# Attention scores on 128 rows in both matmuls, value products that alternate between column halves, and GpSimd's arithmetic on VectorE, in a hybrid decoder layer

## The chip, the cores and the metric

The kernel runs on one core of a Trainium2 chip. The metric is the device time of one execution in microseconds, the median of several runs. Five engines work side by side, each on its own queue of instructions in order: PE (TensorE, with weight loads listed apart as PEld), DVE (VectorE), ACT (ScalarE), POOL (GpSimd) and SP (SyncE, which here only issues DMAs). They meet through semaphores.

## The reference

One decoder layer over 2048 positions of width 1024. After an RMSNorm one projection feeds two groups of heads: four HGRN2 heads (a recurrence in chunks) and eight attention heads of width 64 with two key-value heads, a sliding window of 128 and a learned sink in the softmax. Both outputs are concatenated and projected, then comes a gated MLP with a causal depthwise convolution, then a last RMSNorm. The part that the change touches most:

```python
def sliding_window_attention_with_sinks(q, k, v, sinks):
    qb = q.reshape(B, nb, ATT_BLOCK, ATT_KV_HEADS, ATT_GROUP, ATT_HD)
    kb, vb = band_keys(k), band_keys(v)          # own and previous block of 128 keys
    scores = jnp.einsum('bnqhgd,bnkhd->bnhgqk', qb, kb) * scale
    scores = jnp.where(mask[None, :, None, None], scores, -jnp.inf)
    m = jnp.maximum(jnp.max(scores, axis=-1, keepdims=True), sink)
    p = jnp.exp(scores - m)
    denom = jnp.sum(p, axis=-1, keepdims=True) + jnp.exp(sink - m)
    return jnp.einsum('bnhgqk,bnkhd->bnqhgd', p / denom, vb)
...
proj = rmsnorm(h, norm_mix_w) @ w_in
h = h + jnp.concatenate([o_hg, o_att], -1) @ w_out
v = rmsnorm(h, norm_ffn_w)
h = h + (silu(conv(v @ w_gate)) * (v @ w_up)) @ w_down
return rmsnorm(h, final_norm_w)
```

## The kernel before

The 2048 positions go through in two halves of 1024 (`hf`). Each half has the same stages: the first projections of keys and values, four rounds of heads (in round `h` one HGRN2 head, `hgrn`, and one attention step, `attend`, that handles one query head of each key-value head), the output projection (`out_proj`), gate and up (`gate_up`), and `down`. Activations lie transposed, features on the 128 partitions and positions along the free dimension.

Products with weights keep float32 precision by splitting both factors into a high part that is rounded to the matmul type (a cast on ACT) and the low rest (a subtraction). A product is then high x high, high x low and low x high. The low part of a weight tile is made in `prep` (L177), that of an activation in `split` (L205) and `split_into` (L554). Before the change these subtractions run on POOL unless the caller names VectorE; so do the low part of q (L330) and the gate's product with its sigmoid (L441). A raw weight tile, its high part and its low part turn in rings of three, two and two tiles, so the load, the cast and the subtraction of a tile wait until PE is done with an earlier one.

`unit` (L180) is one projection of 128 output features: 48 matmuls of 512 columns. `project_v` makes the values of two HGRN2 heads with matmuls of 256 columns (`pvv`, L545 to L547).

In `attend`, `qT` holds the 64 features of one query head in partitions 0 to 63 and those of a head of the other key-value group in 64 to 127 (`rows(kv)`). `KS[r, kv]` holds the high part of the keys in the 64 rows of that group and the low part in the other 64. So one matmul with 128 rows, of a `qh` whose high part stands in both halves, gives high x high plus high x low (L341), and a second one with the 64 rows of `ql` and of the high keys gives low x high (L343). A bank of PSUM (`psc`, from the two banks of the kind "at") takes two query blocks of 128, each against 256 keys; ACT copies the previous block's scores out (L350) and VectorE lays the own block's over them under a mask (L351). `qh` is a tile of the ring of raw weights (`RAW` = 3), `ql` one of the ring "pp" (four tiles), which later holds the masked probabilities `po` and `pp`. After the softmax PE transposes the probabilities (L378), VectorE masks them (L381), and the value products (L389 for the own block, L392 for the previous one) write the 64 output features of each key-value head to its own half of PSUM's partitions, so each uses 64 of the array's 128 columns. Their factors are plain float32, and the trace shows two records for each such product. Key-value head 0's eight products come first, then head 1's.

The HGRN2 head ends with a reciprocal root (`rsqrt`, L150 to L160, a chain of a dozen steps on VectorE over 8 elements a partition), a scaling (L520) and a transpose on PE (`pot`, L525).

The order of the instructions on each engine is not the order of the code. A scheduler with a model of the engines' times lays them out when the program is built, within the dependences; after that each engine runs its list in order. So a change of a few lines moves instructions over long stretches. The generators of `hgrn` and `attend`, advanced by the main loop (L949 to L976), give the order that the scheduler starts from.

Of the kernel before, what the change touches and what calls it, by code (L numbers as in the profile page):

```python
# [8 lines left out]
F32 = mybir.dt.float32  # L9
F32R = mybir.dt.float32r  # L10
# [3 lines left out]
ALU = mybir.AluOpType  # L14
# [3 lines left out]
P = 128  # L18
# [27 lines left out]
def hymba_layer(ctx: ExitStack, tc: tile.TileContext, a: dict, out: bass.AP):  # L46
# [122 lines left out]
    def prep(src, slots=False, parts=(slice(0, D),)):  # L169

        raw = raw4(None)
        hi, lo = [hp.tile([P, D], F32R, tag="m", name=f"w{t}", bufs=KT) if slots else
                  wp.tile([P, D], F32R, tag=t, name=f"w{t}", bufs=2) for t in ("hi", "lo")]
        for c in parts:
            nc.sync.dma_start(raw[:, c], src[:, c])
            nc.scalar.copy(hi[:, c], raw[:, c])  # L176
            nc.gpsimd.tensor_tensor(lo[:, c], raw[:, c], hi[:, c].bitcast(F32), op=ALU.subtract)  # L177
        return hi, lo

    def unit(src, X, name, order=range(KT), kind="mm", then={}):  # L180
# [19 lines left out]
    def split(src, w=None, eng=None, dst=None):  # L200

        h, l = dst or new_x()
        if w is None:
            nc.scalar.copy(h, src)
            (eng or nc.gpsimd).tensor_tensor(l, src, h.bitcast(F32), op=ALU.subtract)  # L205
        else:
            nc.scalar.activation(h, src, AF.Identity, scale=w)
            nc.vector.scalar_tensor_tensor(l, src, w, h.bitcast(F32), op0=ALU.mult, op1=ALU.subtract)
        return h, l
# [68 lines left out]
    def rows(kv):  # L278
        return slice(kv * HD, (kv + 1) * HD)
# [32 lines left out]
    def attend(hf, j, X, invb, KS, V, mix, p):  # L312
# [8 lines left out]
        for g in range(NB):  # L321
            sc = p.tile([P, 2, 4, P], F32, tag="sc", name="sc", bufs=2)
            gs = slice(g * 512, (g + 1) * 512)
            qh = wp.tile([P, 2, 512], F32R, tag="raw", name="qh", bufs=RAW)
            ql = p.tile([P, 512], F32R, tag="pp", name="ql", bufs=4)
            for kv in range(2):
                r, other = rows(kv), rows(1 - kv)
                nc.scalar.copy(qh[r, kv], qT[r, gs])
                nc.scalar.copy(qh[other, kv], qT[r, gs])
                nc.gpsimd.tensor_tensor(ql[r], qT[r, gs], qh[r, kv].bitcast(F32), op=ALU.subtract)  # L330
            for i0 in (0, 2):
                for kv in range(2):
                    r = rows(kv)
                    pb = ps("at", "psc")
                    first = hf == 0 and g == 0 and i0 == 0
                    for i in range(2):
                        n = g * 4 + i0 + i
                        w0 = 1 if first and i == 0 else 0
                        o = pb[:, i * 256 + w0 * P:(i + 1) * 256]
                        ks = slice((n + w0) * P, (n + 2) * P)  # L340
                        nc.tensor.matmul(o, qh[:, kv, (i0 + i) * P:(i0 + i + 1) * P], KS[:, kv, ks],  # L341
                                         start=True, stop=False)
                        nc.tensor.matmul(o, ql[r, (i0 + i) * P:(i0 + i + 1) * P], KS[r, kv, ks], start=False, stop=True)  # L343
                    pv = pb.rearrange("p (i w k) -> p i w k", i=2, w=2)
                    dst = sc[:, kv, i0:i0 + 2]
                    if first:
                        nc.vector.memset(dst[:, 0], NEG)
                        nc.scalar.copy(dst[:, 1], pv[:, 1, 0])
                    else:
                        nc.scalar.copy(dst, pv[:, :, 0])  # L350
                    nc.vector.copy_predicated(  # L351
                        dst, C.own.bitcast(U32).unsqueeze(1).to_broadcast([P, 2, P]), pv[:, :, 1])
# [19 lines left out]
        for g, sc in enumerate(scs):  # L372
# [7 lines left out]
                for dst, mk in zip(pm[kv], (C.ownT, C.prevT)):  # L380
                    nc.vector.tensor_tensor(dst, ptv, mk.unsqueeze(1).to_broadcast([P, 4, P]), op=ALU.mult)  # L381
            oT = ps("at", "poT")
            for kv in range(2):
                r = rows(kv)
                po, pp = pm[kv]
                for i in range(4):
                    n = g * 4 + i
                    noprev = hf == 0 and n == 0
                    nc.tensor.matmul(oT[r, i * P:(i + 1) * P], V[:, n + 1, r], po[:, i],  # L389
                                     start=True, stop=noprev)  # L390
                    if not noprev:
                        nc.tensor.matmul(oT[r, i * P:(i + 1) * P], V[:, n, r], pp[:, i],  # L392
                                         start=False, stop=True)
            gs = slice(g * 512, (g + 1) * 512)
            if j < ATT_J - 1:
                nc.scalar.copy(qT[:, gs], oT)
# [9 lines left out]
    def hgrn(hf, h, X, invb, vs, WG, mix, p, fu=None):  # L406
# [28 lines left out]
        def gate():  # L435
            gu = unit(WG.get(h, a["w_g"][h]), X, "g")
            s = p.tile([P, HALF], F32, tag="f", name="sg", bufs=2)
            for b, bs in halves():
                nc.vector.tensor_tensor(q[:, bs], gu[b], invb[:, bs], op=ALU.mult)
                nc.scalar.activation(s[:, bs], q[:, bs], AF.Sigmoid)  # L440
                nc.gpsimd.tensor_tensor(q[:, bs], q[:, bs], s[:, bs], op=ALU.mult)  # L441

        if h == HG - 1:
            gate()
# [106 lines left out]

    def split_into(h, l, src, eng=None):
        nc.scalar.copy(h, src)  # L553
        (eng or nc.gpsimd).tensor_tensor(l, src, h.bitcast(F32), op=ALU.subtract)  # L554

    class Operands:

# [486 lines left out]
```

## Time and profile before

| | us |
|---|---|
| median of three runs | 2345.15 |
| lowest and highest of the three | 2342.76 and 2345.19 |
| the profiled execution, and its span | 2339.59 and 2337.7 |
| mean granted clock of PE | 0.985 |
| heads of the first half, about | 40 to 440 |
| output projection of the first half, about | 440 to 523 |
| gate and up, then down, of the first half | 523 to 940, 940 to 1166 |

A row of the groups gives line, engine, operation, the tile written and the tiles read, the form and the count; behind the first bar the busy time in us and the mean of one in ns; behind the second the idle time of the engine just before such instructions and what ended it. A row of the timeline gives the start and the length in us and the same names; rows of one kind that follow each other closely are merged (`x2`). Matmuls overlap in the array, so how fast they go is read from the distance of their starts, not from their lengths. `128*64` before the form of a matmul is the number of array rows and columns that it uses.

### The profile page before, as it was taken

The numbers are of one execution on the slowest core, as the hardware profiler recorded it, in microseconds if no ns is written. First come the engines' busy times: TensorE is split into PE (matmuls) and PEld (weight loads), VectorE is DVE, ScalarE is ACT, GpSimd is POOL, SyncE is SP. The second block draws the span as 40 slices with busy tenths as digits, with TensorE's granted clock in tenths as the row PEclk, the third lists the DMA queues.
The fourth block names the chain that finished last, engine by engine and source line by source line (L and its number), as shares of the span: only waits on it lengthen the run. The fifth ranks groups of instructions, "written<-read, shape, count | busy, mean of one in ns | idle before, by whom it ended". The sixth has DMA issues, their size and how long they took to land.

```text
span 2337.7 us, 29813 instructions
## 1 busy us (share of the span) xinstructions
PE 2293.0 (98%) x11622; PEld 1907.0 (82%) x11622; DVE 1630.1 (70%) x2307; ACT 1008.1 (43%) x1735; POOL 295.4 (13%) x176
## 2 busy tenths in 40 slices
PE   8999998999999999999999999999999999999997
PEld 6988987877888888888788879878778888888887
DVE  6446465588788887885854463665888788877866
ACT  5334334254444443534633253343554444453353
POOL 3212215041000000000112122151400000000000
PEclk9999998999999999999999999999999999999999
DMA  4001001142232323883630010012323232349743
GB/s 145 19 28 46 10 28 36 51 152 92 86 117 86 126 81 131 333 297 127 214 115 28 19 46 10 28 55 92 116 77 114 98 113 91 117 144 377 246 138 122
DMA packets 87693, 254.19 MB, mean 109 GB/s; under 512 B 10752, under 2 KB 12928, under 8 KB 87552
## 3 DMA queue, kind: packets, MB, share of 16 engines
q1 hardware_dynamic: 85248, 251.17, 31.4%
q8 instruction: 91, 1.49, 0.3%
q10 hardware_dynamic: 2304, 1.12, 0.2%
q14 instruction: 50, 0.41, 0.1%
HBM read 195.10 MB, written 57.15 MB: 108 GB/s over the span
## 4 chain that ended last, share of the span: by engine, by line
PE 93%; DVE 4%; ACT 2%; issue 1%; DMA 1%; POOL 0%; SPq 0%; ACTq 0%; DVEq 0%; POOLq 0%
PE X L656 7%; PE X L658 7%; PE X L657 7%; PE pop L193 6%; PE f L193 4%; PE q L193 4%; PE hq L193 4%; PE Y L656 3%; PE Y L658 3%; PE Y L657 3%; PE g L193 3%; PE pdx L839 3%; PE plev L456 3%; PE pdx L840 3%; PE pdx L841 3%; PE pdy L840 3%
## 5 line engine op out<-in xcount | busy, mean ns | idle before, releaser
L177 POOL TENSOR_TENSOR wlo<-raw,whi 128x1024 fp32r<-128x1024 f32 (+2 forms) x61 | 145.5, 2387 | 1277.6 <-ACT whi L176 1253.3
L553 ACT CAST whi<-raw 128x1024 fp32r<-128x1024 f32 x88 | 92.6, 1053 | 116.2 <-PE X L657 69.7
L656 PE MATMUL X<-T,whi 128*128 128x512 f32 x352 | 138.2, 393 | 2.1 <-ACT u L662 2.1
L657 PE MATMUL X<-T,whi 128*128 128x512 f32 x352 | 137.7, 391 | 0.0
L658 PE MATMUL X<-T,wlo 128*128 128x512 f32 x352 | 137.6, 391 | 0.0
L723 DVE SCALAR_TENSOR_TENSOR y<-ga,cw,y 128x1024 f32<-128x1024 f32 x88 | 112.6, 1280 | 26.8 <-ACT y L721 26.7
L176 ACT CAST whi<-raw 128x1024 fp32r<-128x1024 f32 (+2 forms) x61 | 62.9, 1034 | 123.1 <-issue 33.5
L554 DVE TENSOR_TENSOR wlo<-raw,whi 128x1024 fp32r<-128x1024 f32 x88 | 107.2, 1218 | 3.8 <-PE pinv L248 3.3
L464 DVE TENSOR_TENSOR Q<-Q,F 128x512 f32<-128x512 f32 x48 | 36.2, 755 | 101.9 <-PE plev L456 75.3
L662 ACT COPY u<-X 128x512 f32<-128x512 f32 x88 | 51.4, 584 | 120.0 <-PE X L658 119.7
L554 DVE TENSOR_TENSOR xld<-raw,xhd 128x1024 fp32r<-128x1024 f32 x72 | 81.0, 1133 | 19.4 <-ACT xhd L553 18.8
L553 ACT CAST xhd<-raw 128x1024 fp32r<-128x1024 f32 x72 | 69.6, 977 | 42.4 <-DMA raw<-act0T 16.4
L193 PE MATMUL pop<-XH,wlo 128*128 128x512 f32 x256 | 81.4, 393 | 0.7 <-POOL wlo L177 0.7
L193 PE MATMUL pop<-XL,whi 128*128 128x512 f32 x256 | 81.9, 395 | 0.0
L193 PE MATMUL pop<-XH,whi 128*128 128x512 f32 x256 | 80.7, 398 | 0.2
L656 PEld LDWEIGHTS X<-T,whi 128*128 128x128 f32 x352 | 66.4, 189 | 16.9 <-ACT u L662 3.0
L456 PEld LDWEIGHTS plev<-Q,K 128*128 128x128 f32 x640 | 77.3, 194 | 2.5 <-issue 0.3
L658 PEld LDWEIGHTS X<-T,wlo 128*128 128x128 f32 x352 | 66.5, 189 | 13.9
L657 PEld LDWEIGHTS X<-T,whi 128*128 128x128 f32 x352 | 66.4, 189 | 14.0 <-issue 0.2
L456 PE MATMUL plev<-Q,K 128*128 128x64 f32 x640 | 77.2, 274 | 0.0
L839 PE MATMUL pdx<-xhd,hid 128*128 128x512 f32 x192 | 74.6, 392 | 1.0 <-ACT hid L553 1.0
L656 PE MATMUL X<-T,Sh 128*128 128x512 f32 x176 | 69.6, 396 | 5.3 <-ACT Sh L553 5.3
(348 smaller groups left out, 6871.8 us busy)
## 6 DMA issues: line engine op xcount, KB each, us to landing
wr<-in_w_down SPq DMA_DIRECT2D x90, 512.0 KB, 5.3
raw<-in_w_gate SPq DMA_DIRECT2D x44, 512.0 KB, 3.6
raw<-in_w_up SPq DMA_DIRECT2D x44, 512.0 KB, 3.6
raw<-act0T SPq DMA_DIRECT2D x20, 512.0 KB, 5.7
raw<-act1T SPq DMA_DIRECT2D x20, 512.0 KB, 5.1
act0B<-y SPq DMA_DIRECT2D x33, 256.0 KB, 2.4
act1B<-y SPq DMA_DIRECT2D x33, 256.0 KB, 2.4
raw<-in_w_out SPq DMA_DIRECT2D x16, 512.0 KB, 4.0
```

The source lines that it names most:

```text
L177: nc.gpsimd.tensor_tensor(lo[:, c], raw[:, c], hi[:, c].bitcast(F32), op=ALU.subtract)
L193: nc.tensor.matmul(o[b], w, x[:, bs], start=f, stop=l)
L456: mm = nc.tensor.matmul(pl[:, c * 64:(c + 1) * 64], K[:, c * P:(c + 1) * P], Qv[:, c * nbc:(c + 1) * nbc, 1], start=True, stop=True)
L553: nc.scalar.copy(h, src)
L554: (eng or nc.gpsimd).tensor_tensor(l, src, h.bitcast(F32), op=ALU.subtract)
L656: nc.tensor.matmul(o, wh[:, ws], xh, start=i == 0 and not more, stop=False, skip_group_check=more)
L657: nc.tensor.matmul(o, wh[:, ws], xl, start=False, stop=False, skip_group_check=more)
L658: nc.tensor.matmul(o, wl[:, ws], xh, start=False, stop=i == 3, skip_group_check=more)
L723: nc.vector.scalar_tensor_tensor(y, g[:, w:w + HALF], C.cw[:, ft, w:w + 1], y, op0=ALU.mult, op1=ALU.add)
L839: nc.tensor.matmul(o, wh[:, i, c], ah[:, i, cols], start=f, stop=False, skip_group_check=more)
L840: nc.tensor.matmul(o, wh[:, i, c], al[:, i, cols], start=False, stop=False, skip_group_check=more)
L841: nc.tensor.matmul(o, wl[:, i, c], ah[:, i, cols], start=False, stop=l, skip_group_check=more)
```

## The change

Three edits. In the scores, `qh` and `ql` become tiles of 128 rows with both halves filled, one pair for each key-value head, from the ring "pp"; the low part is copied into the other half by ACT, and both matmuls of a pair take 128 rows. The second one so adds the product of the low parts, which was left out before. The score loop runs over the key-value heads outside and the pairs of query blocks inside. In the value products, the loop over key-value heads becomes the innermost, so products of the two column halves stand next to each other. And all subtractions and products that ran on POOL now run on VectorE; POOL keeps the masks that are made at the start.

```diff
@@ prep
-            nc.gpsimd.tensor_tensor(lo[:, c], raw[:, c], hi[:, c].bitcast(F32), op=ALU.subtract)
+            nc.vector.tensor_tensor(lo[:, c], raw[:, c], hi[:, c].bitcast(F32), op=ALU.subtract)
@@ split
-            (eng or nc.gpsimd).tensor_tensor(l, src, h.bitcast(F32), op=ALU.subtract)
+            (eng or nc.vector).tensor_tensor(l, src, h.bitcast(F32), op=ALU.subtract)
@@ attend, scores
-            qh = wp.tile([P, 2, 512], F32R, tag="raw", name="qh", bufs=RAW)
-            ql = p.tile([P, 512], F32R, tag="pp", name="ql", bufs=4)
             for kv in range(2):
                 r, other = rows(kv), rows(1 - kv)
-                nc.scalar.copy(qh[r, kv], qT[r, gs])
-                nc.scalar.copy(qh[other, kv], qT[r, gs])
-                nc.gpsimd.tensor_tensor(ql[r], qT[r, gs], qh[r, kv].bitcast(F32), op=ALU.subtract)
-            for i0 in (0, 2):
-                for kv in range(2):
-                    r = rows(kv)
+
+                qh, ql = [p.tile([P, 512], F32R, tag="pp", name=n, bufs=4) for n in ("qh", "ql")]
+                nc.scalar.copy(qh[r], qT[r, gs])
+                nc.scalar.copy(qh[other], qT[r, gs])
+                nc.vector.tensor_tensor(ql[r], qT[r, gs], qh[r].bitcast(F32), op=ALU.subtract)
+                nc.scalar.copy(ql[other], ql[r].bitcast(F32))
+                for i0 in (0, 2):
                     pb = ps("at", "psc")
...
-                        nc.tensor.matmul(o, qh[:, kv, (i0 + i) * P:(i0 + i + 1) * P], KS[:, kv, ks],
-                                         start=True, stop=False)
-                        nc.tensor.matmul(o, ql[r, (i0 + i) * P:(i0 + i + 1) * P], KS[r, kv, ks], start=False, stop=True)
+                        for t, qx in enumerate((qh, ql)):
+                            nc.tensor.matmul(o, qx[:, (i0 + i) * P:(i0 + i + 1) * P], KS[:, kv, ks],
+                                             start=t == 0, stop=t == 1)
@@ attend, value products
-            for kv in range(2):
-                r = rows(kv)
-                po, pp = pm[kv]
-                for i in range(4):
-                    n = g * 4 + i
-                    noprev = hf == 0 and n == 0
-                    nc.tensor.matmul(oT[r, i * P:(i + 1) * P], V[:, n + 1, r], po[:, i],
-                                     start=True, stop=noprev)
-                    if not noprev:
-                        nc.tensor.matmul(oT[r, i * P:(i + 1) * P], V[:, n, r], pp[:, i],
-                                         start=False, stop=True)
+            for i in range(4):
+                n = g * 4 + i
+                noprev = hf == 0 and n == 0
+                for prev in range(1 if noprev else 2):
+                    for kv in range(2):
+                        r = rows(kv)
+                        nc.tensor.matmul(oT[r, i * P:(i + 1) * P], V[:, n + 1 - prev, r], pm[kv][prev][:, i],
+                                         start=prev == 0, stop=noprev or prev == 1)
@@ hgrn, gate
-                nc.gpsimd.tensor_tensor(q[:, bs], q[:, bs], s[:, bs], op=ALU.mult)
+                nc.vector.tensor_tensor(q[:, bs], q[:, bs], s[:, bs], op=ALU.mult)
@@ split_into
-        (eng or nc.gpsimd).tensor_tensor(l, src, h.bitcast(F32), op=ALU.subtract)
+        (eng or nc.vector).tensor_tensor(l, src, h.bitcast(F32), op=ALU.subtract)
```

How the scheduler lays this out, at three places. First PE, at the start of the first attention step's scores. Before (`psc_950` and `psc_958` are the banks of key-value heads 0 and 1):

```order
L341 MATMUL psc_950<-KS_425,qh_942 128x128
L343 MATMUL psc_950<-KS_425,ql_943 128x128
L341 MATMUL psc_950<-KS_425,qh_942 128x256
L343 MATMUL psc_950<-KS_425,ql_943 128x256
L341 MATMUL psc_958<-KS_425,qh_942 128x128
L343 MATMUL psc_958<-KS_425,ql_943 128x128
```

The same place of PE with the change (`psc_948` and `psc_956` are the first and second pair of query blocks of key-value head 0):

```order
L341 MATMUL psc_948<-KS_425,qh_942 128x128
L341 MATMUL psc_948<-KS_425,ql_943 128x128
L341 MATMUL psc_948<-KS_425,qh_942 128x256
L341 MATMUL psc_948<-KS_425,ql_943 128x256
L341 MATMUL psc_956<-KS_425,qh_942 128x256
L341 MATMUL psc_956<-KS_425,ql_943 128x256
```

The pairs of `qh` and `ql` stay next to each other; key-value head 1's scores have moved behind 24 matmuls and eight transposes of other work.

Second PE, in the first step's value products. Before (`po_1144` and `pp_1145` belong to key-value head 0, `po_1153` and `pp_1154` to head 1):

```order
L389 MATMUL poT_1162<-po_1144,V_426 64x128
L392 MATMUL poT_1162<-pp_1145,V_426 64x128
L389 MATMUL poT_1162<-po_1153,V_426 64x128 x2
L392 MATMUL poT_1162<-pp_1154,V_426 64x128
L389 MATMUL poT_1162<-po_1153,V_426 64x128
```

With the change (`po_1152` and `pp_1153` are head 0's, `po_1161` and `pp_1162` head 1's; `f0` and `f1` are another unit's accumulators):

```order
L388 MATMUL poT_1170<-po_1152,V_426 64x128
L193 MATMUL f0_1287<-XL_172,whi_1282 128x512
L193 MATMUL f1_1288<-XL_172,whi_1282 128x512
L193 MATMUL f0_1287<-XH_171,wlo_1283 128x512
L193 MATMUL f1_1288<-XH_171,wlo_1283 128x512
L388 MATMUL poT_1170<-po_1161,V_426 64x128
L388 MATMUL poT_1170<-po_1152,V_426 64x128
L388 MATMUL poT_1170<-po_1161,V_426 64x128
L388 MATMUL poT_1170<-pp_1153,V_426 64x128
L388 MATMUL poT_1170<-pp_1162,V_426 64x128
```

The heads alternate from the second product on; the first one stands alone, four matmuls ahead.

Third VectorE, at the end of the third HGRN2 head in the first half, where the `rsqrt` chain (`ms`, `y`, `t`) precedes the transpose on PE. Before:

```order
L422 TENSOR_TENSOR Q_2975<-hg3_2908,f_2847 128x1024
L150 TENSOR_SCALAR ms_2760<-ss_2733 128x8
L153 TENSOR_SCALAR y_2762<-ms_2760 128x8
L154 TENSOR_SCALAR y_2762<-y_2762 128x8
L155 TENSOR_SCALAR ms_2760<-ms_2760 128x8
L158 TENSOR_TENSOR t_2766<-y_2762 128x8
```

With the change (`XL` is the low part of a tile of the mix, `ql` that of q, `wlo` that of a weight):

```order
L418 TENSOR_TENSOR Q_2999<-hg3_2932,f_2871 128x1024
L330 TENSOR_TENSOR ql_3231<-att3_2992,qh_3230 64x512
L205 TENSOR_TENSOR XL_3082<-att0_700,XH_3081 128x1024
L150 TENSOR_SCALAR ms_2784<-ss_2757 128x8
L205 TENSOR_TENSOR XL_3086<-hg1_1398,XH_3085 128x1024
L153 TENSOR_SCALAR y_2786<-ms_2784 128x8
L177 TENSOR_TENSOR wlo_3522<-raw_3520,whi_3521 128x1024
L154 TENSOR_SCALAR y_2786<-y_2786 128x8
L155 TENSOR_SCALAR ms_2784<-ms_2784 128x8
L205 TENSOR_TENSOR XL_3090<-att1_1582,XH_3089 128x1024
L158 TENSOR_TENSOR t_2790<-y_2786 128x8
L177 TENSOR_TENSOR wlo_3516<-raw_3514,whi_3515 128x1024
```

The chain stood alone on VectorE while POOL made these low parts; now they stand between its steps.

## Prediction

> **What bounds the kernel now.** I read the page first, for which engine the end hangs on.
>
> ```profile
> span 2337.7 us, 29813 instructions
> ...
> PE 2293.0 (98%) x11622; PEld 1907.0 (82%) x11622; DVE 1630.1 (70%) x2307; ACT 1008.1 (43%) x1735; POOL 295.4 (13%) x176
> ...
> PE 93%; DVE 4%; ACT 2%; issue 1%; DMA 1%; POOL 0%; SPq 0%; ACTq 0%; DVEq 0%; POOLq 0%
> ```
>
> PE is busy in 98% of the span and makes up 93% of the chain that ended last. The 2% of the chain on other work leaves little to win by shortening a wait; what can be won is PE time itself. A busy PE need not run at its peak, though, so I look at where its matmuls start further apart than matmuls of the same size elsewhere. The stages, by busy time of the engines in three stretches of the first half (columns: length, then PE, PEld, DVE, ACT, POOL busy, granted clock, DMA share, GB/s):
>
> ```profile
> 40.00:400.00 360.00, 352.16 (x2143) 299.04 (x2142) 188.43 (x325) 142.09 (x337) 93.04 (x49) 0.97 0.09 27
> 440.00:523.00 83.00, 81.57 (x381) 66.82 (x380) 57.68 (x81) 40.24 (x72) 28.67 (x16) 1.00 0.37 127
> 523.00:940.00 417.00, 412.65 (x1800) 339.94 (x1799) 344.82 (x448) 185.10 (x268) 7.23 (x4) 0.99 0.31 103
> ```
>
> The heads (first row) have a full PE, while VectorE works 188 of 360 us. Output projection (second row) has VectorE at 69%. Gate and up (third row) have VectorE at 83%, but next to nothing of POOL to hand over. So the change acts in the heads and the output projection, two times each, and there PE is the bound.
>
> **Term A: the scores.** The timeline of PE in one score group of the first head, and just before it the value projection, which has the same width of 256 with 128 rows:
>
> ```profile
> 104.31 0.29 PE L546 MATMUL pvv<-whi,XL 128*128 128x256 f32 x1
> 104.43 0.28 PE L547 MATMUL pvv<-wlo,XH 128*128 128x256 f32 x1
> ...
> 110.18 0.39 PE L341 MATMUL psc<-KS,qh 128*128 128x256 f32 x1
> 110.49 0.38 PE L343 MATMUL psc<-KS,ql 64*128 64x256 f32 x1
> 110.80 0.38 PE L341 MATMUL psc<-KS,qh 128*128 128x256 f32 x1
> 111.12 0.38 PE L343 MATMUL psc<-KS,ql 64*128 64x256 f32 x1
> ```
>
> Nothing waits, yet each start is 0.31 us after the last one, against 0.12 us in the value projection. What differs is that every second matmul takes 64 rows of the array and the next one 128. The groups by form:
>
> ```profile
> L343 PE MATMUL psc<-KS,ql 64*128 64x256 f32 (+1 forms) x128 | 49.4, 386 | 0.0
> L341 PE MATMUL psc<-KS,qh 128*128 128x256 f32 (+1 forms) x128 | 46.9, 366 | 0.0
> ```
>
> 256 matmuls, none of which the edit adds or removes: after it both of a pair have 128 rows. 16 of them are only 128 wide. 240 x (0.31 - 0.12) = 45.6 us. A few tenths for entering a group (they come in pieces of four or eight between other work) take some of it back; I take **43 us**. Bounds: 48 if the narrow ones gain as well, 37 if every group pays 0.1 to 0.2 us at its edges or waits for its two PSUM banks. The extra product, low part of q with low part of k, fills rows that stood empty and costs no column.
>
> **Term B: the value products.** The timeline of PE in the first head's value products:
>
> ```profile
> 141.38 0.38 PE L392 MATMUL poT<-pp,V 128*64 128x128 f32 x2
> 141.60 0.38 PE L389 MATMUL poT<-po,V 128*64 128x128 f32 x2
> 141.82 0.38 PE L392 MATMUL poT<-pp,V 128*64 128x128 f32 x2
> ...
> 142.25 0.27 PE L392 MATMUL poT<-pp,V 128*64 128x128 f32 x1
> 142.31 0.27 PE L389 MATMUL poT<-po,V 128*64 128x128 f32 x1
> 142.36 0.27 PE L392 MATMUL poT<-pp,V 128*64 128x128 f32 x1
> 142.42 0.27 PE L389 MATMUL poT<-po,V 128*64 128x128 f32 x1
> ```
>
> Two records (one fp32 product) take 0.22 us where one half of the columns works alone, 0.11 us a record. Around 142.3, where the last products of key-value head 0 meet the first of key-value head 1, a record starts every 0.055 us: the two halves run side by side. The change makes all of it such a meeting.
>
> ```profile
> L389 PE MATMUL poT<-po,V 128*64 128x128 f32 x256 | 45.5, 278 | 0.0
> L392 PE MATMUL poT<-pp,V 128*64 128x128 f32 x240 | 43.5, 273 | 0.0
> ```
>
> 496 records at 0.109 are 54 us; at 0.055 they are 27. Some already overlap, and the new program still puts single value products between other matmuls where the second key-value head's masked scores come later. I take **20 us**; bounds 0 and 27.
>
> A weight load in that overlapped stretch:
>
> ```profile
> 142.25 0.14 PEld L392 LDWEIGHTS poT<-pp,V 128*64 128x64 f32 x1
> ```
>
> It runs while records of both halves are under way. The Trainium skill, "TensorE: Matmul & The Clock Gate", section "Part 3: Packing small matmuls — row/col tiling", says that a weight load overlaps with running matmuls only where the row group differs. Both halves here use the same 128 rows, so by that rule term B would be 0 and not 20; the row above speaks against it.
>
> **Term C: one stall.** Of PE's waits in the heads one is long. VectorE, POOL and PE at that place, from their timelines, and the granted clock behind it from the busy times:
>
> ```profile
> 380.21 2.26 DVE L160 SCALAR_TENSOR_TENSOR y<-t,y 128x8 f32<-128x8 f32 x1
> 384.80 0.17 DVE L159 TENSOR_TENSOR t<-t,ms 128x8 f32<-128x8 f32 x1
> ...
> 380.11 2.33 POOL L177 TENSOR_TENSOR wlo<-raw,whi 128x1024 fp32r<-128x1024 f32 x1
> ...
> 385.95 1.32 PE L525 MATMUL pot<-ident,on 128*128 128x128 f32 x5 [7.84 <-DVE on L520]
> ...
> 386.00:396.00 10.00, 10.00 (x32) 7.70 (x33) 3.23 (x6) 2.74 (x4) 4.66 (x2) 0.50 0.19 59
> ```
>
> An 8-element VectorE step takes 2.26 us beside a POOL instruction and 0.17 without one; a chain of such steps makes PE wait 7.84 us, and for 10 us and more behind it the clock is 0.50, worth some 5 us. With POOL idle the steps are short. But their place is taken: in the new order four 1024-wide subtractions of the mix and three weight subtractions stand on VectorE before or inside this chain, 7 x 1.22 = 8.5 us, and the projection's first matmuls, ahead of this transpose on PE, wait for four of them. So part of the stall stays: I take **9 us** of the 13, bounds 0 and 13.
>
> **Term D: the clock in the heads.** Six stretches of 3.4 us right behind score groups run at half clock; the first and the last:
>
> ```profile
> 214.40:217.80 3.40, 3.40 (x9) 2.72 (x9) 1.84 (x3) 0.37 (x1) 0.00 (x0) 0.51 0.48 154
> ...
> 1484.20:1487.60 3.40, 3.40 (x9) 2.54 (x10) 3.26 (x8) 1.82 (x3) 0.00 (x0) 0.50 0.00 0
> ```
>
> Each costs about 1.7 us, 10 us in all. Denser scores should make some of them go; I take **5 us**, bounds 0 and 10.
>
> **Term E: what VectorE and ACT take on.**
>
> ```profile
> L177 POOL TENSOR_TENSOR wlo<-raw,whi 128x1024 fp32r<-128x1024 f32 (+2 forms) x61 | 145.5, 2387 | 1277.6 <-ACT whi L176 1253.3 <-PE g L193 24.2
> L330 POOL TENSOR_TENSOR ql<-att,qh 64x512 fp32r<-64x512 f32 x32 | 44.6, 1393 | 58.9 <-ACT qh L328 57.3
> ...
> L554 DVE TENSOR_TENSOR wlo<-raw,whi 128x1024 fp32r<-128x1024 f32 x88 | 107.2, 1218 | 3.8 <-PE pinv L248 3.3 <-PE X L658 0.3 <-ACT whi L553 0.2
> L554 DVE TENSOR_TENSOR S<-raw,S 128x512 fp32r<-128x512 f32 x44 | 30.3, 689 | 14.8 <-ACT S L553 14.7
> ...
> L329 ACT CAST qh<-att 64x512 fp32r<-64x512 f32 x32 | 19.8, 619 | 0.8
> ```
>
> The same subtraction takes 2387 ns on POOL and 1218 on VectorE, half; 1393 becomes at most 689. So POOL's 295 us become at most some 150 on VectorE: 1780 of about 2270, 78%. In the heads 188 + 47 = 235 of some 325 us, in the output projection 58 + 14 = 72 of 83, 87%, less what POOL no longer slows. The third ACT copy of each q adds 32 x 0.62 = 20 us on an engine that is 39% busy in the heads. PE's work hides both as long as nothing that PE needs stands behind a late subtraction: on VectorE's queue a weight subtraction waits for ACT's cast, which waits for PE to free a ring slot, and behind it stand PSUM reads that PE needs. On POOL nothing stood behind it. In return q leaves the ring of three raw weight tiles, so loads on SP's queue no longer wait for score matmuls; its four tiles a group now turn in the ring of the masked scores, where a tile is freed by work several microseconds of PE earlier. I take **4 us of new waits**; bounds 5 us gained (POOL's hold on VectorE gone elsewhere) and 25 lost.
>
> **The sum.** 43 + 20 + 9 + 5 - 4 = 73 us. The profiled execution took 2339.6 us (2 beyond its span), the median of the three runs is 2345.2; 73 off these is 2267 and 2272. I give **2271**, close to the median's.
>
> **The rivals.** A row of PE's groups that bears on the first:
>
> ```profile
> L193 PE MATMUL pop<-XH,wlo 128*128 128x512 f32 x256 | 81.4, 393 | 0.7 <-POOL wlo L177 0.7
> ```
>
> 1. *VectorE takes POOL's place in PE's waits.* For it: 87% in the output projection, the order in term C. Against it: 0.7 us is all that PE waited for POOL's weights in the output projection, and half the duration arrives earlier even from a busier queue. Price: term C is 0, D is 0, and at the ends of both last heads and both output projections 3 to 6 us appear, some 18: 43 + 20 - 18 = 45, so **2300**.
> 2. *The halves do not overlap beyond the short meeting seen*: a half's weight load waits until the other half's matmul has ended. The row of the weight load under term B and the starts 0.055 us apart speak against it. B is 0, **2291**. The Trainium skill's rule named there, in "TensorE: Matmul & The Clock Gate", is of this kind.
> 3. *The scores keep their spacing*, since it comes from changing the stationary operand and not from the rows: A is 0, **2314**. The value projection changes it each time at 0.12 us, which speaks against it.
> 4. *Slower.* Every weight subtraction becomes a wait on VectorE's queue in front of a PSUM read. 44 of them lie in the heads of the two halves; from 1.8 us of PE idle for each (44 x 1.8 = 79) the gain is gone, at 2 us the time is **2353**. VectorE's 27% of free time in the heads, and PE's two accumulator pairs ahead, speak against it.
>
> **How the numbers follow.** Forecast 72%, rivals 14, 6, 4 and 4. All low bounds together (48 + 27 + 13 + 10, and E even) give 2247; the first two rivals end at 2300. The range 2247 to 2300 leaves out the third and fourth and a little more. Runs of this kernel differ by 0.1%, so 0.2% (5 us) is about what can be told from no change. Faster: everything but the fourth and a share of the third, 94%; same 2%; slower 4%.
>
> **What would show it.** A: score matmuls starting 0.12 us apart. B: value records 0.055 us apart throughout a group. C: the wait of the transpose under 4 us, 8-element steps at 0.17 us everywhere. D: fewer half-clock stretches behind scores. E: VectorE under 80% in the heads, POOL empty. It would be wrong if the waits of PE for VectorE summed to tens of microseconds, or if the spacing of either kind of matmul stayed.

## The result, and the profile after

| | us |
|---|---|
| before, median of the runs beside it (2342.76 to 2345.19) | 2345.08 |
| changed, median of four runs (2254.99 to 2256.36) | 2255.0 |
| ratio, with its 95% interval | 0.962 [0.9603, 0.9636] |
| span of the profiled execution, before and changed | 2337.7 and 2253.3 |

The change makes the kernel 3.8% faster, 90 us by the medians. The two profiled executions lie 84.4 us apart, because the one of before was among the quicker ones of its kernel; the accounts below add up to 84.4. Two later comparisons gave 0.9629 [0.9614, 0.9643] and 0.9632 [0.9614, 0.965].

From the page of the changed kernel, the span, the busy times and the chain that ended last:

```profile
span 2253.3 us, 29743 instructions
PE 2216.0 (98%) x11622; PEld 1863.3 (83%) x11622; DVE 1639.7 (73%) x2456; ACT 1021.8 (45%) x1763; POOL 6.0 (0%) x27
PE 94%; DVE 4%; DMA 1%; ACT 1%; issue 0%; SPq 0%; DVEq 0%; ACTq 0%
```

PE has the same 11622 records and is still the bound, with 77 us less busy time: the records stand closer together. POOL's 295 us are gone, but VectorE, which took over 149 instructions, is busy only 10 us longer.

The same three stages of the first half as in the prediction, at their new places (columns as there):

```profile
40.00:365.00 325.00, 323.98 (x2185) 284.49 (x2184) 200.92 (x376) 149.29 (x354) 0.00 (x0) 1.00 0.11 35
399.00:481.00 82.00, 80.90 (x381) 66.72 (x380) 55.74 (x98) 41.30 (x74) 0.00 (x0) 1.00 0.38 129
481.00:896.00 415.00, 411.87 (x1803) 338.89 (x1802) 342.82 (x450) 184.67 (x267) 0.00 (x0) 0.99 0.31 104
```

The heads have lost the most, and their granted clock is 1.00 where it was 0.97. From the start of `gate_up` in one kernel to that in the other, the heads and output projection of the first half are 41.7 us shorter, `down` of the first half with the heads and output projection of the second 38.3; gate and up give 2.8 and 1.7, and the rest nothing.

PE's timeline in the first group of scores:

```profile
106.34 0.28 PE L341 MATMUL psc<-KS,ql 128*128 128x256 f32 x1
106.46 0.28 PE L341 MATMUL psc<-KS,qh 128*128 128x256 f32 x1
106.58 0.28 PE L341 MATMUL psc<-KS,ql 128*128 128x256 f32 x1
106.69 0.28 PE L341 MATMUL psc<-KS,qh 128*128 128x256 f32 x1
```

Starts are 0.12 us apart, where they were 0.31. PE's timeline in a group of value products (rows merge two key-value heads, each the lower or the upper half of the columns):

```profile
215.46 0.44 PE L388 MATMUL poT<-pp,V 128*64 128x128 f32 x4
215.68 0.44 PE L388 MATMUL poT<-po,V 128*64 128x128 f32 x4
215.89 0.44 PE L388 MATMUL poT<-pp,V 128*64 128x128 f32 x4
```

Four records in 0.22 us are 0.055 a record, half of the 0.11 of before. The scores, by their form:

```profile
L341 PE MATMUL psc<-KS,qh 128*128 128x256 f32 (+1 forms) x128 | 33.7, 293 | 0.0
L341 PE MATMUL psc<-KS,ql 128*128 128x256 f32 (+1 forms) x128 | 32.2, 281 | 0.0
```

Both now have 128 rows. These lengths overlap, so the gain is in the starts. The 256 score records, each from its start to the next one's, without waits and with half of the time at half clock taken off, sum to 75.7 us before and 31.7 after. The 496 value records, from start to start as they are: 53.9 before, 34.3 after.

PE's waits, before (first fence) and after (second), in total, how many, and the longest:

```profile
PE pot L525 <- DVE on L520: 9.3, 2, 7.8
PE X L656 <- ACT Sh L553: 5.3, 2, 2.6
```

```profile
PE plev L452 <- DVE K L461: 5.8, 4, 2.7
PE X L652 <- ACT whi L549: 2.9, 2, 2.0
PE X L652 <- ACT Sh L549: 2.3, 2, 1.1
```

The transpose `pot` no longer waits. But PE has got a new wait for VectorE, some 12 us of program later, before the recurrence's `plev`. Its place in the first half on PE, and the stretches behind it in the first and the second half:

```profile
366.93 2.00 PE L452 MATMUL plev<-Q,K 128*128 128x64 f32 x16 [0.88 <-DVE K L461]
371.62 0.66 PE L452 MATMUL plev<-Q,K 128*128 128x64 f32 x2 [2.69 <-DVE K L461]
```

```profile
371.20:378.00 6.80, 6.38 (x30) 6.27 (x31) 5.89 (x13) 4.50 (x23) 0.00 (x0) 0.50 0.01 2
1480.60:1497.60 17.00, 16.57 (x66) 14.62 (x66) 14.55 (x30) 7.04 (x35) 0.00 (x0) 0.50 0.00 1
```

VectorE's timeline ahead of the longer wait, without a gap between its instructions:

```profile
367.88 0.72 DVE L437 TENSOR_TENSOR hg<-hg,sg 128x512 f32<-128x512 f32 x1
...
369.05 1.22 DVE L353 TENSOR_REDUCE m<-sc 128x8 f32<-128x1024 f32 x1
370.19 0.68 DVE L460 TENSOR_TENSOR Q<-Q,F 128x512 f32<-128x512 f32 x1
370.79 0.69 DVE L461 TENSOR_TENSOR K<-K,F 128x512 f32<-128x512 f32 x1
```

The first row is a product that ran on POOL before. So the stall has moved on to the next point where VectorE is late, and its half clock with it.

### The profile page after: what moved, and what is told of

The parts are those of the page before. It is cut to its first block, busy times and chain, and to the rows that moved or that the text cites. A ratio compares the mean times of both kernels' runs of the same rounds, so it can differ in the third digit from the quotient of the medians.

```text
span 2253.3 us, 29743 instructions
## 1 busy us (share of the span) xinstructions
PE 2216.0 (98%) x11622; PEld 1863.3 (83%) x11622; DVE 1639.7 (73%) x2456; ACT 1021.8 (45%) x1763; POOL 6.0 (0%) x27
## 4 chain that ended last, share of the span: by engine, by line
PE 94%; DVE 4%; DMA 1%; ACT 1%; issue 0%; SPq 0%; DVEq 0%; ACTq 0%
PE X L652 7%; PE X L653 7%; PE X L654 7%; PE pop L193 6%; PE hq L193 4%; PE q L193 4%; PE f L193 4%; PE g L193 4%; PE pdx L835 4%; PE pdx L836 4%; PE pdx L837 4%; PE Y L652 3%; PE Y L653 3%; PE Y L654 3%; PE plev L452 3%; PE pdy L836 3%
## 5 line engine op out<-in xcount | busy, mean ns | idle before, releaser
L452 PEld LDWEIGHTS plev<-Q,K 128*128 128x128 f32 x640 | 82.6, 205 | 8.8 <-DVE K L461 4.0
L452 PE MATMUL plev<-Q,K 128*128 128x64 f32 x640 | 83.2, 286 | 5.8 <-DVE K L461 5.8
L177 DVE TENSOR_TENSOR wlo<-raw,whi 128x1024 fp32r<-128x1024 f32 (+2 forms) x61 | 72.9, 1201 | 7.2 <-ACT whi L176 7.1
L836 PE MATMUL pdx<-xld,hid 128*128 128x512 f32 x192 | 74.8, 390 | 0.0
```

The lines of the kernel that those rows point to most:

```text
L177: nc.vector.tensor_tensor(lo[:, c], raw[:, c], hi[:, c].bitcast(F32), op=ALU.subtract)
L452: mm = nc.tensor.matmul(pl[:, c * 64:(c + 1) * 64], K[:, c * P:(c + 1) * P], Qv[:, c * nbc:(c + 1) * nbc, 1], start=True, stop=True)
L836: nc.tensor.matmul(o, wh[:, i, c], al[:, i, cols], start=False, stop=False, skip_group_check=more)
```

## The experiments

The theory was that of the prediction: the scores gain from equal rows, the value products from overlapping halves, and moving POOL's work shortens VectorE's steps. The rivals were that one of the three brings nothing by itself, or that their gains do not simply add. Batches ran on different chips, each beside runs of the kernel before: its median was 2342.95 (19 runs, 2332.72 to 2350.91) for the first four kernels.

**The scores alone**, with the subtraction left on POOL:

```diff
+                qh, ql = [p.tile([P, 512], F32R, tag="pp", name=n, bufs=4) for n in ("qh", "ql")]
...
+                nc.gpsimd.tensor_tensor(ql[r], qT[r, gs], qh[r].bitcast(F32), op=ALU.subtract)
+                nc.scalar.copy(ql[other], ql[r].bitcast(F32))
...
+                        for t, qx in enumerate((qh, ql)):
+                            nc.tensor.matmul(o, qx[:, (i0 + i) * P:(i0 + i + 1) * P], KS[:, kv, ks],
```

> The score edit alone on the kernel before (128 rows in both matmuls, POOL keeps its arithmetic). Theory: every change between 64 and 128 rows costs 0.19 us, so 240 pairs' worth of it, about 46 us, goes: 2299 us. If the half-clock stretches behind score groups come from the thin matmuls there, they go as well (10 us more): 2289 us, and fewer than two of the six are left in the heads. Rival, that these stretches come from POOL's hold on VectorE: the six stay and the time is 2299 us or above.

2290.06 us, ratio 0.9778 [0.9749, 0.9807]: 53 us. The clock in the heads of the first half (the row of windows) is full, and the wait of the transpose has grown:

```profile
40.00:355.00 315.00, 313.19 (x2076) 276.64 (x2074) 170.22 (x310) 141.50 (x336) 75.53 (x41) 1.00 0.11 34
```

```profile
PE pot L524 <- DVE on L519: 15.4, 2, 7.7
```

All six short half-clock stretches behind score groups went with the thin groups alone, while POOL still worked. One of 3.4 us at the start of the second half (1183.8 us in the kernel before, 1158.8 here) stayed; it stands behind the matmuls of one column that sum the squares (`pst`), not behind scores. The 7.7 us wait, which before stood in the first half only (9.3 in both), now stands in both: PE arrives earlier, VectorE does not.

**The value products alone:**

```diff
+            for i in range(4):
...
+                for prev in range(1 if noprev else 2):
+                    for kv in range(2):
```

> The order of the value products alone on the kernel before. Theory: the halves overlap all through a group, records 0.055 us apart, 20 us less: 2325 us. Rival, that only a short meeting of the halves overlaps: records stay 0.109 us apart but for a few, 2340 to 2345 us.

2330.15 us, 0.9947 [0.9928, 0.9967]: 13 us. The starts of the value records are 34.2 us in sum, 19.7 less than before. The remaining 7 went into the clock: the trace's stretches at half clock add up to 86.4 us where the kernel before had 70.6, and half of such time is lost. In the heads of the first half:

```profile
40.00:375.00 335.00, 333.63 (x2096) 282.31 (x2094) 176.90 (x307) 133.25 (x327) 81.79 (x44) 0.98 0.08 26
```

**The engine alone:**

```diff
-            nc.gpsimd.tensor_tensor(lo[:, c], raw[:, c], hi[:, c].bitcast(F32), op=ALU.subtract)
+            nc.vector.tensor_tensor(lo[:, c], raw[:, c], hi[:, c].bitcast(F32), op=ALU.subtract)
```

and the four other places likewise.

> Only the arithmetic of POOL moves to VectorE; scores and value products as before. Theory: the 7.84 us wait in front of the transpose of the first half goes with the slow clock behind it, little else changes on PE: 2325 to 2335 us; VectorE's busy time rises by a few us only (POOL's hold on it was worth nearly what it takes on), so about 1640 us. Rival, that VectorE becomes what PE waits for: 2345 us or above and waits of PE for VectorE of over 20 us.

2336.61 us, 0.9974 [0.9956, 0.9991]: 6 us, just short of the range expected. VectorE is busy 1641.3 us, as expected. PE's wait for the transpose is gone, and one that was not expected, for a later product of VectorE, stands in its place, though PE's scores are as slow as before:

```profile
PE plev L456 <- DVE K L465: 5.9, 4, 2.3
```

PE's waits fell by some 7 us in all, but its time at half clock rose from 70.6 to 81.7 us.

The single edits bring 53 + 13 + 6 = 72 us; together they bring 84 to 90. Each single gain has an interval of 4 to 7 us to either side; the run with POOL's arithmetic back, below, shows more clearly that they do not add.

**Half of the changes of rows.** The kernel before, with the pair of every second query block turned round, so that the order is high, low, low, high:

```diff
-                        nc.tensor.matmul(o, qh[:, kv, (i0 + i) * P:(i0 + i + 1) * P], KS[:, kv, ks],
-                                         start=True, stop=False)
-                        nc.tensor.matmul(o, ql[r, (i0 + i) * P:(i0 + i + 1) * P], KS[r, kv, ks], start=False, stop=True)
+                        cs = slice((i0 + i) * P, (i0 + i + 1) * P)
+                        for t, (x, y) in enumerate(((qh[:, kv, cs], KS[:, kv, ks]), (ql[r, cs], KS[r, kv, ks]))[::1 - 2 * i]):
+                            nc.tensor.matmul(o, x, y, start=t == 0, stop=t == 1)
```

> The kernel before, but in every second query block the matmul with the 64 rows of the low part comes first, so that two matmuls of one kind stand next to each other. Same matmuls, half the changes of rows. Theory that the change of rows costs: four matmuls take 2 x 0.12 + 2 x 0.31 = 0.86 us and not 1.25, some 24 us less: 2321 us. Rival, that a 64-row matmul itself, or its new stationary operand, is slow: starts stay 0.31 us apart, 2345 us.

2310.18 us, 0.9864 [0.9834, 0.9894]: 33 us, more than expected. PE's timeline in a group:

```profile
110.21 0.28 PE L343 MATMUL psc<-KS,qh 128*128 128x256 f32 x1
110.42 0.50 PE L343 MATMUL psc<-KS,ql 64*128 64x256 f32 x2
110.85 0.50 PE L343 MATMUL psc<-KS,qh 128*128 128x256 f32 x2
111.28 0.50 PE L343 MATMUL psc<-KS,ql 64*128 64x256 f32 x2
```

Two records take 0.43 us: one step of 0.31 where the rows change and one of 0.12 where they do not. The matmuls, their operands and their number are those of before, so the change of the stationary operand (rival 3) is not what cost; the change between 64 and 128 rows is, 0.19 us each. The clock gains as well: the half-clock stretches add up to 56.4 us, 14 less than before, and none of the six short ones in the heads is left. In the traces the score records give 20 us and the clock 7, together the 27 us between the two spans (2337.7 and 2310.7). The other 6 of the 33 us come from which executions were profiled: that of before was 3 us under its median here, this one 2 above its own.

The second batch ran beside a median of 2342.49 (7 runs), with the changed kernel in it again.

> The changed kernel again, beside the three that follow, to compare them on one chip: 2255 us, 90 us under the kernel before.

2256.28 us (2254.16 to 2259.54).

**The order of the two heads in the value products**, in the changed kernel:

```diff
-                    for kv in range(2):
+                    for kv in (1, 0):
```

> The changed kernel, but the value products begin with key-value head 1, whose masked scores are ready last, so that no first product stands alone between other matmuls. Theory: each entry into and exit from the 64-column form costs PE about 0.1 us; a lone product takes 0.36 us where it takes 0.06 us in the group. Some ten of these go: 2 to 4 us less than the changed kernel. Rival: the products of the group now wait for head 1's mask as a whole and PE idles instead, no gain or a loss.

2251.07 us (2248.70 to 2252.83), 0.9605 [0.959, 0.9619]: 5.2 us below the changed kernel beside it. With head 0 first, its first product becomes ready before head 1's probabilities are masked, and the scheduler puts it alone between other matmuls; PE then pays 0.36 us for two records. With head 1 first, both heads are ready together: lone pairs of records at 0.36 us or more fall from twelve to one, and the value records sum to 30.9 us instead of 34.3. That is 3.4 of the 5.2 us.

**How far PE looks ahead.** In the changed kernel, blocks of four records of one half of the columns, then four of the other:

```diff
-                for prev in range(1 if noprev else 2):
-                    for kv in range(2):
+                for kv in range(2):
+                    for prev in range(1 if noprev else 2):
```

> The changed kernel, but the two products of a query block (own and previous keys, four records) stay together for each column half: the halves alternate in blocks of four records and not of two. Theory that the next half's work starts as soon as it is the next in the queue and the other half is only a record or two behind: three of four records stand alone, 0.08 us a record, some 10 us more than the changed kernel. Rival that PE looks many records ahead: no difference.

2257.6 us, 0.9637 [0.9621, 0.9653], no different from the changed kernel: that expectation missed. PE's timeline:

```profile
214.96 0.44 PE L388 MATMUL poT<-pp,V 128*64 128x128 f32 x4
215.18 0.44 PE L388 MATMUL poT<-po,V 128*64 128x128 f32 x4
```

Four records every 0.22 us, as in the changed kernel: the halves still run side by side. (The value records sum to 36.2 us, 1.9 more, since more of them stand in small pieces between other matmuls; the times can't tell this from nothing.) PE must begin a matmul of the other half while four records of the first stand ahead of it.

**Blocks of eight** (third batch, beside 2340.05 from 7 runs):

```diff
+            for i0 in (0, 2):
+                for kv in range(2):
+                    r = rows(kv)
+                    for i in (i0, i0 + 1):
...
+                        for prev in range(1 if noprev else 2):
```

> The changed kernel, but the column halves alternate in blocks of eight records (two query blocks). Blocks of four overlapped wholly, and in the kernel before, with blocks of 14 to 16 records, only about four records of each half overlapped where the halves meet. Theory that PE starts work about four records ahead of the one that is held up: half of the records overlap, 0.08 us a record and some 8 us more than the changed kernel. Rival, that it looks eight or more ahead: no difference, and the short overlap of before comes from something else (the second half's mask was late).

2268.54 us, 0.9688 [0.9665, 0.9712], some 12 us more than the changed kernel in its own comparisons. Its value records sum to 42.3 us, 8 more than in the changed kernel, as the theory had it; the rest lies in waits and the clock (some 3 and 2 us more in the trace). From the end of a group:

```profile
216.79 0.44 PE L389 MATMUL poT<-po,V 128*64 128x128 f32 x4
217.01 0.44 PE L389 MATMUL poT<-pp,V 128*64 128x128 f32 x4
217.29 0.38 PE L389 MATMUL poT<-po,V 128*64 128x128 f32 x2
217.51 0.38 PE L389 MATMUL poT<-pp,V 128*64 128x128 f32 x2
```

First four records in 0.22 us, then, with only one half left, two. A group of 32 takes 2.5 us, between the 1.9 of the run with blocks of four and the 3.21 of the kernel before: about half of it overlaps. With these block lengths the overlap reaches about four records ahead. The halves need not alternate record by record, but eight in a row are too many.

**POOL's arithmetic back on POOL** in the changed kernel (both matmul edits stay; second batch):

```diff
-            nc.vector.tensor_tensor(lo[:, c], raw[:, c], hi[:, c].bitcast(F32), op=ALU.subtract)
+            nc.gpsimd.tensor_tensor(lo[:, c], raw[:, c], hi[:, c].bitcast(F32), op=ALU.subtract)
```

and the four other places likewise.

> The changed kernel with POOL's arithmetic back on POOL (both matmul edits stay). Sum of the two edits alone: 2345 - 53 - 13 = 2279 us. Theory that the move of the arithmetic is worth more beside the denser scores, since VectorE's chain in front of the transpose then makes PE wait in both halves (15 us and the slow clock behind): 2272 to 2280 us, so 17 us or more above the changed kernel. Rival, that the move is worth 6 us as it was alone: 2261 us.

2285.26 us (2284.26 to 2285.94), 0.9751 [0.9736, 0.9765]. So the engine's move is worth 29 us beside the matmul edits, though 6 by itself. That is the way the theory had it, and 5 us beyond its range. The wait of the transpose, and the chain ahead of it on VectorE and POOL:

```profile
PE pot L521 <- DVE on L516: 18.5, 2, 9.7
```

```profile
343.98 2.40 POOL L205 TENSOR_TENSOR XL<-att,XH 128x1024 fp32r<-128x1024 f32 x1
344.07 2.33 DVE L154 TENSOR_SCALAR y<-y 128x8 int32<-128x8 int32 x1
346.32 0.16 DVE L155 TENSOR_SCALAR ms<-ms 128x8 f32<-128x8 f32 x1
346.33 1.29 POOL L330 TENSOR_TENSOR ql<-att,qh 64x512 fp32r<-64x512 f32 x1
346.44 5.84 DVE L158 TENSOR_TENSOR t<-y 128x8 f32<-128x8 f32 x1
347.59 2.36 POOL L205 TENSOR_TENSOR XL<-hg,XH 128x1024 fp32r<-128x1024 f32 x1
349.92 2.33 POOL L177 TENSOR_TENSOR wlo<-raw,whi 128x1024 fp32r<-128x1024 f32 x1
352.31 0.17 DVE L159 TENSOR_TENSOR t<-t,ms 128x8 f32<-128x8 f32 x1
```

An 8-element product on VectorE takes 5.84 us: it starts beside the first of three subtractions of POOL, and ends where the third ends. The denser PE arrives at the transpose in both halves while this chain still runs: 18.5 us of waits against 9.3 before, and 76.2 us at half clock against 47.7 in the changed kernel. Over all of PE's list the waits are 22 us longer, and outside the waits the half clock costs 9 us more; together they make up the 30 us between the spans.

**Only the mix's low parts on POOL**, twelve subtractions that stand next to that chain (third batch):

```diff
-                        M[kt] = split(mix[kt])
+                        M[kt] = split(mix[kt], eng=nc.gpsimd)
```

> The changed kernel, but the low parts of the six mix tiles (twelve subtractions of 128x1024 in all, at the end of the last head of each half) go back to POOL; everything else stays on VectorE. Theory that POOL slows VectorE about as much as it relieves it: VectorE's busy time falls by less than the 14.6 us (12 x 1.22) that it hands over, by 2 us or even not at all, its small steps beside a POOL instruction take 2 us again, PE's waits at that place do not fall below the 5.8 us of the changed kernel and the time is 2255 us or up to 10 us above. Rival that VectorE is simply too full there: 6 us of waits and the slow clock behind them go, 2240 to 2245 us.

2262.08 us (2261.85 to 2263.57), 0.9663 [0.9636, 0.9691], some 6 us more than the changed kernel's 2256 in its own comparisons (this batch had no run of it, and the intervals of the ratios just touch). POOL's two groups of them, PE's wait, and the busy times:

```profile
L205 POOL TENSOR_TENSOR XL<-att,XH 128x1024 fp32r<-128x1024 f32 x6 | 15.8, 2629 | 0.0
L205 POOL TENSOR_TENSOR XL<-hg,XH 128x1024 fp32r<-128x1024 f32 x6 | 15.4, 2562 | 1441.3 <-DVE y L160 1093.3 <-ACT XH L204 348.0
```

```profile
PE pot L521 <- DVE on L516: 7.3, 2, 3.8
```

```profile
PE 2217.4 (98%) x11622; PEld 1864.9 (83%) x11622; DVE 1644.5 (73%) x2444; ACT 1021.7 (45%) x1763; POOL 37.7 (2%) x39
```

VectorE gave up twelve instructions (14.6 us in the changed kernel) and is busy 5 us longer, as the theory had it: beside POOL six of the chain's small steps take over 2 us again. The rival, that VectorE is now too full near the transpose and would be helped, falls; what counts there is whether POOL works at the same time.

**The variant against both kernels** (fourth batch, beside 2340.59 from 9 runs): the kernel with head 1 first again, and the changed kernel.

> The variant whose value products begin with key-value head 1, once more beside the changed kernel, since the intervals of the two touched in the first comparison: 2251 us, 4 to 5 us under the changed kernel. If the first difference was chance: within 2 us of it.

> The changed kernel on the same chip as the variant above: 2255 to 2256 us.

2251.18 (2249.77 to 2252.20), 0.961 [0.9594, 0.9627], and 2256.69 (2253.31 to 2258.84). In both comparisons the variant is 5.2 to 5.5 us below the changed kernel and the runs do not overlap; it beats both kernels.

## Why the prediction was right, point by point

Predicted 2271 in 2247 to 2300, measured 2255. The sum of 73 came out as 84.4 in the profiled executions; the other 6 us to the medians are the quick profiled run of before. A and B, 63 of the 73, held in size and in mechanism. That the total is near as well is in part luck: C was put some 11 us too high, D and E 5 and 13 too low.

**A, the scores: right.** Predicted 43, measured 75.7 - 31.7 = 44, at 0.12 us a record as forecast. The mirrored pairs show the cause: changing from 64 to 128 rows and back, not the operand. Rival 3 falls.

**B, the value products: right.** Predicted 20, measured 53.9 - 34.3 = 19.6. Rival 2 falls. The Trainium skill's rule in "TensorE: Matmul & The Clock Gate", section "Part 3: Packing small matmuls — row/col tiling", that a weight load overlaps running matmuls only where the row group differs, does not hold here: both halves use the same 128 rows, and with blocks of four, too, a record starts every 0.055 us. The lone products that the prediction allowed for cost what the other order of the heads gets back, 3.4 of its 5 us by the value records.

**C, the one stall: the step that failed.** Predicted 9 of 13 us. Before, the transpose's waits were 9.3 us, and of the 17.1 us at half clock at the long one 12.9 lay behind it, 4.2 within it: 9.3 + 6.4 = 15.7 us. After, the waits before `plev` are 5.8 us, and of the stretches of 6.8 and 17.1 us at half clock all but 0.9 lie outside them: 5.8 + 11.5 = 17.3. Measured against before, C is worth nothing, or a little less. The steps of the chain did become short, as said: before, 16 of the 221 steps of all the `rsqrt` chains took over 1 us, after, none took more than 0.17. The prediction asked what else would stand in front of the transpose, and not which of VectorE's products would be the next to be late with the moved work in its queue. It is above all the moved work that makes `plev` wait: 5.9 us with the engine alone, where PE was no faster, against 0.4 with the scores alone. Denser matmuls have a part in it too: 2.7 with the value products alone, 3.5 with both matmul edits and POOL's arithmetic back. Nor did the prediction see that the matmul edits alone would have doubled the stall (18.5 us with POOL's work back), so that the engine's move keeps 29 us rather than winning 9.

**D, the clock in the heads: right in kind, too small.** Predicted 5 of 10. All six short stretches behind score groups went: 6 x 3.4 / 2 = 10 us. Both the scores alone and the mirrored pairs show that it is the score groups with alternating rows that brought the clock down; neither the value products nor the engine's move removes these stretches. Whether it is the change of rows or only the thinner work of such a group, no run separates.

**E, what VectorE takes on: wrong in sign.** Predicted 4 us lost, measured about 9 gained: half-clock stretches at the start of the gates went from 17 to 10.2 us (3.4 us), the one behind `pst` at the start of the second half went (1.7 us; it stays in every run with all of POOL's arithmetic on POOL), and PE's waits other than for the transpose and `plev` fell from 26.9 to 23.0. Behind it stands the mis-sized load: VectorE was to be 1780 us busy and is 1640. The prediction subtracted "what POOL no longer slows" without a number. One of VectorE's groups with two factors in SBUF and one that reads PSUM, before and after:

```profile
L225 DVE TENSOR_TENSOR invb<-invb,sq 128x512 f32<-128x512 f32 x28 | 33.7, 1242 | 2.8 <-ACT sq L223 2.3
L590 DVE TENSOR_TENSOR h<-pop,xres 128x512 f32<-128x512 f32 x32 | 20.7, 684 | 10.9 <-PE pop L193 10.8
```

```profile
L225 DVE TENSOR_TENSOR invb<-invb,sq 128x512 f32<-128x512 f32 x28 | 18.0, 683 | 0.0
L586 DVE TENSOR_TENSOR h<-pop,xres 128x512 f32<-128x512 f32 x32 | 20.8, 686 | 18.0 <-PE pop L193 17.0 <-DMA xres<-in_xT 0.9
L177 DVE TENSOR_TENSOR wlo<-raw,whi 128x1024 fp32r<-128x1024 f32 (+2 forms) x61 | 72.9, 1201 | 7.2 <-ACT whi L176 7.1
```

The moved instructions cost 139 us on VectorE (72.9 for the weights; the other 88 go by their own groups), yet its busy time rose by 10: some 130 us were time in which POOL held VectorE's own instructions, those that read two operands from SBUF and the small ones, not those that read PSUM. In the trace of before, sorted by whether POOL works meanwhile, the first row's instructions took 680 ns alone (12 of them) and 1805 beside POOL (14), the second row's 686 (19) and 680 (9). The Trainium skill, "GPSIMD Engine Reference", "1. Specifications", says that the two engines share SBUF interfaces and collide where VectorE's instruction has two SBUF inputs or runs in a two-port mode; the row with two such inputs agrees. Steps with one input were held too (L154 above, 2.33 us), and the trace doesn't tell their mode. That POOL no longer holds VectorE is why rival 1 came only in part: C fell to nothing as it said, but D did not, nor did its 18 us of waits appear. The output projection's VectorE is busy 55.7 of 82 us, 68% and not 87, and the heads' 200.9 of 325, 62% and not 72.

A + B + C + D + E = 44 + 19.6 - 1.6 + 10 + 9 = 81 of the 84.4; the last 3 us are spread over PE's other matmuls. What stays open is how long the half clock behind the new wait lasts: after the same waits of 0.9 and 2.7 us in the first half it was 6.8 us in two profiled executions of the changed kernel and 13.7 in a third. No run took the wait of `plev` away.

Three slips in the prediction's own figures change nothing above. It takes PE's idle 2% for the chain's share on other work, which its row puts at 7%; its fourth rival, 44 waits of 2 us, comes to 2356 from the median, not 2353; and its noise of 0.1% comes from three runs, where later ones differ by 0.8%.

## What to carry to other kernels

Do not alternate matmuls of 64 and of 128 rows: fill the empty rows, or at least put equal ones side by side; the starts tell, not the lengths. Let products that use half of the columns take turns within some four records, and have both halves' inputs ready before the first is issued. Elementwise work on POOL isn't free while VectorE works through a chain of small steps on which PE waits, and such a chain weighs more the faster PE becomes: price edits together, since their gains need not add.

## What the runs showed of the hardware

A change between 64 and 128 rows costs 0.19 us of start distance (matmuls of 256 columns), and a PE that is busy all through such a group still fell to half clock for 3.4 us behind it, six times in the heads of before, and not once with equal rows or with half as many changes. Overlapping the column halves alone did not help against that: 86.4 us at half clock against 70.6.

An instruction on 8 elements of VectorE took 0.16 us alone and 5.84 beside three of POOL's subtractions in a row.

The time of the kernel before varies with its clock: its 19 runs lay between 2332.72 and 2350.91, 0.8%, at mean clocks of 0.981 to 0.988. The changed kernel's runs in one comparison lay within 0.25%.
